# The last layer's output projection over pairs of token tiles: seven block products in place of eight

## The chip, the cores and the metric

The kernel runs on one core of one Trainium2 chip. The metric is the device time of one execution in microseconds (us), as the median of several executions. The core has five engines that run their own instruction streams and meet only at semaphores: TensorE (PE; PEld is its weight load), VectorE (DVE), ScalarE (ACT), GpSimd (POOL) and SyncE (SP), which here issues every DMA. Each engine works through its instructions in program order.

## The reference

Two layers of a streaming encoder over 2048 tokens of width 1024, and a final normalisation:

```python
for layer in range(2):
    hn = rms_norm(x, norm_gain[layer])
    aq, ak, av, ag, rq, rk, rv, rg = split(hn @ w_in[layer])      # eight parts of 512
    ya = chunked_rel_attention(aq, ak, av, rel_bias[layer])       # 8 heads x 64, band of 9 chunks of 64
    yr = chunkwise_retention(rq, rk, rv, cos, sin)                # 4 heads x 128, a running state
    y = concat([ya * silu(ag), yr * silu(rg)])
    x = x + y @ w_out[layer]                                      # the output projection: 2048x1024 by 1024x1024
return rms_norm(x, final_gain)
```

The change concerns `x + y @ w_out[layer]` of the second layer, and the final `rms_norm` that follows it.

## The kernel before

**Numbers in two halves.** Every matmul operand is split into two float16 halves, an upper one and the rest. A product takes three matmuls: upper by upper, upper by rest, rest by upper. ACT writes the upper half (a copy with a scale), DVE the rest (value times scale minus upper half).

**Stages.** For each layer and each of four head groups `s`, and each of four blocks `n` of 512 tokens, `dense_T` (L654) and `dense_V` (L785) project the input; the attention and retention of a block run beside the dense work of the next block. The generator `attention` (L823) has 24 steps; `run` (L1219) takes one of them for each step of the dense work, and spreads background work (`push`, `bg`) over the same steps: loading and splitting the next weights, for instance. The results of attention and retention go to `y_d` in device memory by tiles of 128 tokens. All four computing engines have their order written out by hand (`manual_schedule`); the SP queue's order is made by the framework, apart from DMAs marked `in_turn`.

**The output projection, `wout` (L1117).** It runs after the last dense block. The work goes over 16 token tiles of 128 rows, each in two halves of 512 output columns; one half is 8 blocks of 128 inner rows by three terms, 24 matmuls into one PSUM bank of the pool `psD` (two banks):

```python
for m in range(8 * (i % 3), 8 * (i % 3) + 8):
    kt, w = divmod(m, 3)
    h_, w_ = ((u.h, gc[c].vh), (u.h, gc[c].vl), (u.lo, gc[c].vh))[w]
    pe.matmul(ps, h_[:, kt, :], w_[:, kt, :], start=(m == 0), stop=(m == 23))
```

Six steps make a tile. After each half DVE adds PSUM times a scale to the residual tile (L1175). Ahead of that, a tile's `y` is loaded (`y_load` L967, SP), squared on ACT for its scale (`y_squares` L990), scaled by five small DVE operations (`y_scale` L999, `norm_scale`), split by `rows_hi` (ACT, L234) and `rows_lo` (DVE, L240), and transposed by two DMAs, one for each half (`y_turn` L1005, `transpose_rows` L243 and L244). POOL takes no part in this. `final` (L1013) does the last normalisation of a tile: squares on ACT (L212), a power on POOL (L219), a multiply on DVE (L1018) and the store (L1019). The last half of the last tile is cut into two quarters of 256 columns (L1159), finished by `final_half` (L1073). While the first tiles are projected, the last block's attention still runs, one of its 24 steps for each step of `wout`. The weights are split by `prep_O` (L551), once for each half of the columns, and the first tile's `y` is prepared by `wout_first` (L1096), all as background work of the last dense blocks.

Of the kernel before, what the change touches and what calls it, by code (L numbers as in the profile page):

```python
# [18 lines left out]
P = 128  # L19
# [8 lines left out]
def hybrid_trunk(ctx: ExitStack, tc: tile.TileContext, x, pos, gain, gcol, w_in, w_out, rel, fgain,  # L28
# [1161 lines left out]


    bg = []
    tab_done = set()

    def push(gen, steps):
        bg.append([gen, steps])
# [21 lines left out]

    def run(gen, att, thirds):  # L1219
        left = thirds  # L1220
        for _ in gen:
# [216 lines left out]
    for l in range(DEPTH):  # L1438
        gO = [Grp(), Grp()]
        go = Grp()  # L1440
        for s in range(NSW):
            g = grp(l, s)
            for n in range(NS):
# [25 lines left out]
                if n == (NS - 1 if (l, s) == (0, 0) else 1):  # L1469
                    if s + 1 < NSW:  # L1470
                        push(prep_T(l, s + 1, grp(l, s + 1)), 25 if (l, s) != (0, 0) else 19)
                    else:
# [6 lines left out]
                if last:  # L1479
                    us = []  # L1480
                    push(wout_first(l, go, us), 9)
                if not first:
                    run(dT, att, 12 if last else 10 if n == 0 else 18 if (l, s, n) == (0, 0, NS - 1) else 22 if (l, s) == (0, 0) else 24)
                if n == NS - 1:
                    if s + 1 < NSW:
                        push(prep_V(l, s + 1, grp(l, s + 1)), 23)
                    else:
                        push(with_turn(prep_O(l, 1, gO[1], go), us), 12)
# [8 lines left out]
        if l + 1 == DEPTH:  # L1497
            ring["fg"] = b3.tile([P, D], F32, tag="wh", name="fg")
            sp.dma_start(ring["fg"], fgain.to_broadcast([P, D]))
        wT = Sections(l + 1, 0, grp(l + 1, 0), True) if l + 1 < DEPTH else None  # L1500
        wo = wout(l, go, gO, us, wT)
# [78 lines left out]
```

## Time and profile before

| what | value |
|---|---|
| median of 3 runs | 2060.24 us (2058.01 to 2061.81) |
| span of the profiled execution | 2060.7 us |
| PE busy | 1999.4 us, 97% |
| DVE busy | 1228.1 us, 60% |
| ACT busy | 1134.8 us, 55% |
| POOL busy | 688.1 us, 33% |
| DMA, share of 16 engines, main queue | 65.6% |

The profiled execution's own time and its span are taken as one: 2060.7 us, which is 0.5 us (0.02%) above the median of the runs and inside their range.

How to read the rows: a group of instructions is given as line, engine, operation, output<-inputs, shape, count, then busy time in us and the mean ns of one, then the idle time of the engine in front of them. A row of the stretches of time gives for each engine its busy us and, in brackets, its instructions; then the granted TensorE clock, the DMA share and GB/s. A row of the timeline or of the chain starts with the time in us from the start of the span, then the duration. PE durations overlap: matmuls are pipelined, so that the distance of two starts is what one costs in a row of many.

### The profile page before, as it was taken

Reading aid. Unit: us, or ns where it says so; the run is one execution under the profiler, and the core shown is the slowest. Engines: PE = TensorE matmul, PEld = TensorE weight load, DVE = VectorE, ACT = ScalarE, POOL = GpSimd, SP = SyncE. Lnnn points to the kernel's source line nnn. Section 1 sums busy time; section 2 is a strip of 40 time slices with the busy share of each in tenths; the row PEclk is TensorE's granted clock in tenths of the full one; section 3 lists DMA queues with packets and bytes.
Section 4 is the critical chain, followed back from the end, with each engine's and each line's share of the span. In section 5 each row is a group of like instructions: output and inputs, shape, how many; then the busy total and the mean of one; then the engine's idle time right before and its main releaser. Section 6 shows DMA issues by size and latency. Waiting matters only on the chain. (4 is left out here: it accounts for less than half of the span.)

```text
span 2060.7 us, 39339 instructions
## 1 busy us (share of the span) xinstructions
PE 1999.4 (97%) x14038; PEld 1052.9 (51%) x14038; DVE 1228.1 (60%) x3804; ACT 1134.8 (55%) x2526; POOL 688.1 (33%) x701
## 2 busy tenths in 40 slices
PE   6988999999999999999999999999999999999998
PEld 4444555555555555554444555555555555555544
DVE  6776666565556555666553556555655566557643
ACT  6556665556565645555444546655656565455432
POOL 0344343434334434430003443444333334333100
PEclk9999999999999999999999999999999999999999
DMA  8778664547584754899774546554746775658864
GB/s 227 169 161 178 155 148 109 112 114 164 117 185 113 165 128 101 174 209 263 219 185 113 124 104 156 116 126 103 158 117 150 148 155 124 129 115 187 224 203 139
DMA packets 645701, 313.64 MB, mean 152 GB/s; under 512 B 459232, under 2 KB 602080, under 8 KB 645504
## 3 DMA queue, kind: packets, MB, share of 16 engines
q1 hardware_dynamic: 645504, 311.12, 65.6%
q8 instruction: 110, 1.80, 0.4%
q14 instruction: 87, 0.71, 0.1%
HBM read 123.26 MB, written 41.98 MB: 80 GB/s over the span
## 5 line engine op out<-in xcount | busy, mean ns | idle before, releaser
L855 POOL TENSOR_TENSOR pq<-sc,pq 128x640 f16<-128x640 f32 (+4 forms) x256 | 319.4, 1248 | 860.5 <-ACT pq L854 443.8
L852 ACT ACTIVATE sc<-sc,mq,cT 128x640 f32<-128x640 f32 (+4 forms) x256 | 218.4, 853 | 615.6 <-DVE rl L871 309.7
L797 PE MATMUL dV<-whV,hTh 128*128 128x512 f16 x1024 | 353.9, 381 | 7.3 <-DVE gt L815 6.1
L797 PE MATMUL dV<-whV,hTl 128*128 128x512 f16 x1024 | 353.8, 381 | 0.0
L797 PE MATMUL dV<-wlV,hTh 128*128 128x512 f16 x1024 | 353.8, 381 | 0.0
L778 PE MATMUL dT<-hTh,whT 128*128 128x512 f16 x1008 | 346.6, 379 | 2.7 <-DVE kk L697 1.3
L778 PE MATMUL dT<-hTl,whT 128*128 128x512 f16 x1008 | 346.6, 379 | 0.0
L778 PE MATMUL dT<-hTh,wlT 128*128 128x512 f16 x1008 | 346.6, 379 | 0.0
L797 PEld LDWEIGHTS <-hTh 128*128 128x128 f16 x2048 | 197.0, 98 | 224.7 <-DVE gt L815 10.0
L778 PEld LDWEIGHTS <-whT 128*128 128x128 f16 x2016 | 192.1, 98 | 207.7 <-issue 1.6
L849 DVE CUSTOM_DVE_ANT_0 sc<-S,bias 128x640 f32<-128x640 f32 (+4 forms) x256 | 188.3, 735 | 88.8 <-PE S L846 87.4
L1172 PE MATMUL dO<-whO,yly 128*128 128x512 f16 x504 | 191.0, 379 | 1.7 <-DMA yly<-hTl 1.1
L1172 PE MATMUL dO<-whO,yhy 128*128 128x512 f16 x504 | 191.0, 379 | 1.0 <-DMA yhy<-hTh 1.0
L1172 PE MATMUL dO<-wlO,yhy 128*128 128x512 f16 x504 | 191.0, 379 | 0.0
L854 ACT ACTIVATE pq<-sc 128x640 f16<-128x640 f32 (+4 forms) x256 | 171.5, 670 | 8.1
L797 PEld LDWEIGHTS <-hTl 128*128 128x128 f16 x1024 | 99.4, 98 | 112.4 <-issue 3.9
L1172 PEld LDWEIGHTS <-yhy 128*128 128x128 f16 x1008 | 98.1, 98 | 113.7 <-DMA yhy<-hTh 1.5
L778 PEld LDWEIGHTS <-wlT 128*128 128x128 f16 x1008 | 97.2, 98 | 113.7 <-issue 6.0
L845 PE MATMUL S<-k,q 128*128 128x128 f16 (+3 forms) x592 | 142.4, 267 | 0.0
L865 PE MATMUL o<-v,pT 128*128 128x65 f16 x1120 | 129.8, 193 | 6.4 <-DMA pT<-pq 5.5
L866 PE MATMUL o<-v,pT 128*128 128x64 f16 x1120 | 130.1, 195 | 0.0
L846 PE MATMUL S<-k,q 128*128 128x128 f16 (+3 forms) x592 | 129.7, 267 | 0.0
(359 smaller groups left out, 3476.5 us busy)
## 6 DMA issues: line engine op xcount, KB each, us to landing
q<-qq SPq DMA_DIRECT2D x128, 128.0 KB, 2.4
yyy<-y_d SPq DMA_DIRECT2D x32, 512.0 KB, 4.5
stT<-in_w_in_dram SPq DMA_DIRECT2D x27, 512.0 KB, 4.8
stV<-in_w_in_dram SPq DMA_DIRECT2D x26, 512.0 KB, 4.6
k<-kk SPq DMA_DIRECT2D x128, 64.0 KB, 2.0
swp<-rot SPq DMA_DIRECT2D x64, 128.0 KB, 3.1
tabc<-tab SPq DMA_DIRECT2D x32, 256.0 KB, 3.0
tabs<-tab SPq DMA_DIRECT2D x32, 256.0 KB, 3.1
```

The lines of the kernel that those rows point to most:

```text
L778: pe.matmul(ps, w_[:, j, kt, :], h_[:, kt, :], start=(m == 0), stop=(m == 23))
L797: pe.matmul(ps, h_[:, kt, a * P:(a + 1) * P], w_[:, kt, :], start=(m == 0), stop=(m == 23))
L845: pe.matmul(o, st.q[:, hx, 0, cs], k_, start=True, stop=False)
L846: pe.matmul(o, st.q[:, hx, 1, cs], k_, start=False, stop=True)
L849: dve.tensor_tensor_reduce(out=v, in0=S[:, 0:w], in1=g.bias[hx][:, 640 - w:640], scale=1.0, scalar=-3.0e38, op0=ALU.add, op1=ALU.max, accu ...
L852: act.activation(v, v, AF.Exp, bias=m[:, 0:1], scale=g.c[:, 0:1])
L854: act.activation(pq[:, 0:w], v, AF.Copy)
L855: pool.tensor_tensor(pq[:, w:2 * w], v, pq[:, 0:w], op=ALU.subtract)
L865: pe.matmul(o[:, 0:65], u.p[:, b, :], v_[:, 0:65], start=(b == 0), stop=False)
L866: pe.matmul(o[:, 0:64], u.p[:, b, :], v_[:, 65:129], start=False, stop=False)
L1172: pe.matmul(ps, h_[:, kt, :], w_[:, kt, :], start=(m == 0), stop=(m == 23))
```

## The change

The last layer no longer uses `wout`. Two token tiles make a pair: 256 rows, cut into two by two blocks A11, A12, A21, A22 (128 tokens by 512 inner columns). `w_out` is cut into two by two blocks of 512 by 512. Seven products of sums of such blocks replace the eight block products; each is 4 inner blocks by 3 terms, 12 matmuls of 128x512, so a pair takes 84 in place of 96. The sums of blocks are made in float32 before they are split into halves.

- `fast_weights` and a part of `pair_first` make seven weight blocks in place of four: sums and differences on POOL, then the split on ACT and DVE. The weights are loaded 12 times 512 KB in place of 8 times.
- `pair_first` prepares the first pair as background work of the last dense block, in 24 steps.
- `fast_out` runs 8 pairs, each in 12 rounds of 7 matmuls. In the same rounds it prepares the next pair by the list `plan`: squares, scales, multiplication in place (ACT, float32), five sums of blocks (POOL), and for each of seven blocks the upper half (`pair_rows`, ACT), the rest (`pair_lower`, DVE, one of them on POOL) and one DMA transpose of both halves (`pair_turn`). The row buffers are three tags used in turn.
- Each product goes into one or two of the four output blocks: `add_to` is the DVE operation as before; `by_copy` is a scaled copy on ACT and an addition on POOL.
- The attention that runs beside it takes one step for every second round (`run(..., 96, 2)`).

```diff
+    PRODS = (("A22", "D21"), ("A11", "D12"), ("S2", "B11"), ("S5", "B22"), ("S1", "T1"), ("S7", "T7"), ("S6", "T6"))
+    def fast_weights(l, fw, go):
...
+        for j in range(4):
...
+                st += load_sec(w_out[l, :, c * 512 + j * P:c * 512 + (j + 1) * P], f"F{l}_{j}{c}")
...
+                pool.tensor_tensor(tm[:, k * h:(k + 1) * h], st[0][:, k * h:(k + 1) * h], st[1][:, h:KT], op=ALU.add)
...
+            pool.tensor_tensor(st[0][:, h:KT], st[0][:, h:KT], st[0][:, 0:h], op=ALU.subtract)
+            pool.tensor_tensor(st[1][:, 0:h], st[1][:, 0:h], st[0][:, 0:h], op=ALU.add)
...
+    def pair_sq(u, k, junk):
...
+        act.activation(junk, u.y[k], AF.Square, accum_out=m)
...
+    def pair_mul(u, k):
+        act.activation(u.y[k], u.y[k], AF.Copy, scale=u.s[k][:, 0:1])
...
+    SUMS = {"S1": ("A11", "A22", ALU.add), "S2": ("A21", "A22", ALU.add), "S6": ("A21", "A11", ALU.subtract),
+            "S7": ("A12", "A22", ALU.subtract), "S5": ("A11", "A12", ALU.add)}
...
+        pool.tensor_tensor(part_of(u, nm), part_of(u, a), part_of(u, b), op=op)
+    def pair_rows(u, nm, space=None):
+        if space is None:
+            tag = ("tabc", "tabs", "swp")[rowring[0] % 3]
...
+        act.activation(space[:, 0:512], part_of(u, nm), AF.Copy)
+    def pair_lower(u, nm):
+        eng = pool if nm == "S1" and u.p else dve
+        eng.tensor_tensor(u.r[nm][:, 512:1024], part_of(u, nm), u.r[nm][:, 0:512], op=ALU.subtract)
+    def pair_turn(u, nm):
+        sp.dma_start_transpose(out=u.T[nm], in_=u.r[nm])
...
+    def fast_out(l, fw, go, u, areas):
...
+        mm = [(i, kt, w) for i in range(7) for kt in range(KT // 2) for w in range(3)]
+        plan = {0: (("sq", 0),), 1: (("sq", 1), ("scale", 0)), 2: (("scale", 1), ("mul", 0)), 3: (("mul", 1), ("rows", "A11")),
+                4: (("lower", "A11"), ("rows", "A22"), ("sum", "S2")),
+                5: (("turn", "A11"), ("lower", "A22"), ("rows", "S2"), ("sum", "S1"), ("sum", "S6")),
+                6: (("turn", "A22"), ("lower", "S2"), ("sum", "S7"), ("sum", "S5")),
+                7: (("turn", "S2"), ("rows", "S5")), 8: (("lower", "S5"), ("rows", "S1"), ("x", 0)),
+                9: (("turn", "S5"), ("lower", "S1"), ("rows", "S7"), ("y", 0)),
+                10: (("turn", "S1"), ("lower", "S7"), ("rows", "S6"), ("y", 1)),
+                11: (("turn", "S7"), ("lower", "S6"), ("turn", "S6"))}
...
+            def add_to(x_, c, ps, s_):
+                dve.scalar_tensor_tensor(out=half(x_, c), in0=ps, scalar=s_[:, 0:1], in1=half(x_, c), op0=ALU.mult,
+                                         op1=ALU.add)
+            def by_copy(x_, c, ps, s_, op):
...
+                act.activation(v, ps, AF.Copy, scale=s_[:, 0:1])
+                pool.tensor_tensor(half(x_, c), half(x_, c), v, op=op)
...
+                    pe.matmul(ps, u.T[an][:, kt + (4 if w == 2 else 0), :], fw.w[bn][1 if w == 1 else 0][:, kt, :],
+                              start=(m % 12 == 0), stop=(m % 12 == 11))
...
+                    if i == 0:
+                        add_to(x2, 0, ps, s2)
+                        by_copy(x1, 0, ps, s1, ALU.add)
+                    elif i == 1:
+                        add_to(x1, 1, ps, s1)
+                        by_copy(x2, 1, ps, s2, ALU.add)
+                    elif i == 2:
+                        add_to(x2, 0, ps, s2)
...
+                        by_copy(x2, 1, ps, s2, ALU.subtract)
+                    elif i == 3:
+                        add_to(x1, 1, ps, s1)
+                        by_copy(x1, 0, ps, s1, ALU.subtract)
+                    elif i == 4:
+                        add_to(x1, 0, ps, s1)
+                        add_to(x2, 1, ps, s2)
+                    elif i == 5:
+                        add_to(x1, 0, ps, s1)
+                        final(u.t, x1, at)
+                    else:
+                        add_to(x2, 1, ps, s2)
+                        final(u.t + 1, x2, at)
...
-    def run(gen, att, thirds):
+    def run(gen, att, thirds, slow=1):
...
-            if att[0] is not None and next(att[0], att) is att:
+            if att[0] is not None and i % slow == 0 and next(att[0], att) is att:
...
+                if (l + 1, s, n) == (DEPTH, NSW - 1, 2):
+                    push(fast_weights(l, fw, go), 24)
...
+                        push(pair_first(l, u0, fw, go, areas), 24)
...
+            run(fast_out(l, fw, go, u0, areas), att, 96, 2)
+            continue
```

The last product of the last pair is cut into two quarters of 256 columns with `final_half`, as the last half was before. `final` puts its three operations into later rounds (2, 3 and 5 rounds after the last addition); those that fall behind the last round are issued after everything else.

More of the change, by code (lines that the diff above doesn't have):

```diff
@@ L1497, in hybrid_trunk @@
         if l + 1 == DEPTH:
-            ring["fg"] = b3.tile([P, D], F32, tag="wh", name="fg")
+            ring["fg"] = cp.tile([P, D], F32, tag="gb", name="fg")
             sp.dma_start(ring["fg"], fgain.to_broadcast([P, D]))
+            run(fast_out(l, fw, go, u0, areas), att, 96, 2)
+            continue
         wT = Sections(l + 1, 0, grp(l + 1, 0), True) if l + 1 < DEPTH else None
```

225 lines of the change are left out of this document (220 added, 5 removed).

## Prediction

> **What bounds the kernel now.** I read the page's busy times first, then stretches of time, the chain of work that ended last, and the timelines of single engines around the projection. The chain's last long piece and the stretches carry the argument.
>
> ```profile
> 1820.00:1874.00 54.00, 54.00 (x414) 29.08 (x413) 33.54 (x96) 32.86 (x69) 23.68 (x19) 1.00 0.68 135
> 1876.20:1936.70 60.50, 60.18 (x468) 32.41 (x466) 43.02 (x127) 33.47 (x67) 17.40 (x18) 1.00 0.93 219
> 1936.80:2049.00 112.20, 112.20 (x522) 50.95 (x521) 48.69 (x106) 33.48 (x50) 6.02 (x11) 1.00 0.65 190
> ```
>
> ```profile
> 1936.74 112.25 PE dO L1172 x520
> ```
>
> ```profile
> 1873.60 0.38 PE L797 MATMUL dV<-wlV,hTh 128*128 128x512 f16 x1
> ...
> 1876.25 0.38 PE L1172 MATMUL dO<-whO,yhy 128*128 128x512 f16 x1
> ```
>
> The stretches are, in order, the last dense block, the projection with attention beside it, and the projection alone. PE (first column after the length) is full in all three, DVE, ACT and POOL (third to fifth) are not, and the clock is 1.00. So PE is the bound of the projection, and what one matmul costs is 112.25 us / 520 = 0.216 us. It runs from 1876.25 to 2054.2 us, where the tail (quoted below) begins: 178 us. Of this 744 x 0.216 + 48 quarter matmuls x 0.11 (half of 0.216) = 166 us are its own, so 12 us are attention's. Two tiles cost 96 x 0.216 = 20.7 us.
>
> **What the change removes.** 12 of 96 matmuls in each of 8 pairs: 96 x 0.216 = 20.7 us of PE. A pair becomes 84 x 0.216 = 18.1 us. That is the whole possible gain, if PE stays the bound.
>
> **What it adds to the other engines.** Prices, ACT first (timeline; then one line's instructions with minimum, median and maximum in ns):
>
> ```profile
> 1958.24 1.15 ACT L234 ACTIVATE hTh<-yyy,sy 128x1024 f16<-128x1024 f32 x1 [4.68 <-DVE iy L153]
> 1961.78 1.03 ACT L212 ACTIVATE fj<-hTl 128x1024 f32<-128x1024 f32 x1 [2.39 <-DVE hTl L1175]
> ...
> 1962.84 1.04 ACT L997 ACTIVATE hTh<-yyy 128x1024 f16<-128x1024 f32 x1
> ```
>
> ```profile
> L711 ACT ACTIVATE raw<-dT x32: 571/597/597, 54.2 to 1847.9; 128x512 f32<-128x512 f32 x32
> ```
>
> ```profile
> L724 ACT ACTIVATE rot<-raw x32: 612/613/631, 81.7 to 1870.5; 128x512 f16<-128x512 f32 x32
> ```
>
> In a row of ACT instructions a 1024-wide square costs 1.06 us from start to start, so about 0.1 us of each overlaps the next; a scaled 1024-wide copy 1.05, a 512-wide copy out of PSUM 0.6, a 512-wide float16 row 0.52 (0.61 alone).
>
> POOL and DVE:
>
> ```profile
> 1851.21 1.27 POOL L719 TENSOR_TENSOR rot<-rot,tabc 128x512 f32<-128x512 f32 x1 [1.88 <-PE S L846]
> 1852.44 1.28 POOL L720 TENSOR_TENSOR swp<-swp,tabs 128x512 f32<-128x512 f32 x1
> 1853.79 1.27 POOL L721 TENSOR_TENSOR rot<-rot,swp 128x512 f32<-128x512 f32 x1
> ...
> 1864.74 2.26 POOL L719 TENSOR_TENSOR raw<-raw,tabc 128x512 f32<-128x512 f32 x1
> ```
>
> ```profile
> L727 DVE TENSOR_TENSOR rot<-raw,rot x32: 678/1423/1477, 82.4 to 1871.1; 128x512 f16<-128x512 f32 x32
> ```
>
> ```profile
> L1018 DVE SCALAR_TENSOR_TENSOR hTl<-hTl,rsf,fg x7: 1274/1277/2318, 1926.2 to 2050.8; 128x1024 f32<-128x1024 f32 x7
> ```
>
> ```profile
> L1175 DVE SCALAR_TENSOR_TENSOR hTh<-dO,oscy,hTh 128x512 f32<-128x512 f32 x16 | 12.0, 750 | 32.0 <-PE dO L1172 32.0
> ```
>
> ```profile
> L219 POOL TENSOR_TENSOR rsf<-ssf,mhalf 128x1 f32<-128x1 f32 x15 | 8.2, 547 | 107.5 <-DVE ssf L217 107.5
> ```
>
> A 512-wide float32 addition on POOL takes 1.27 us, three of them one behind the other 3.8. `pair_lower` has the form of L727: 0.68 us undisturbed, but mostly 1.4; L719 and L1018 also have a long form, 1.0 us longer. These are the times when DVE and POOL both work on SBUF and one waits for the other. `add_to` is L1175, 0.75.
>
> The DMAs (issue to landing in us, first beside attention, then alone):
>
> ```profile
> yyy<-y_d SPq DMA_DIRECT2D x6, 512.0 KB, 3.9
> ...
> yhy<-hTl SPq DMA_TRANSPOSE x2, 3.7
> ```
>
> ```profile
> yyy<-y_d SPq DMA_DIRECT2D x8, 512.0 KB, 4.4
> ...
> yhy<-hTl SPq DMA_TRANSPOSE x5, 3.1
> ```
>
> ```profile
> 1960.76 1.23 SPq L243 DMA_TRANSPOSE yhy<-hTh  x1
> ```
>
> SP is held for 1.23 us by each transpose.
>
> Sums of busy time for a pair of `fast_out`: POOL 10 additions x 1.27 + 2 powers x 0.55 = 13.8 us. ACT 4 squares, 2 multiplications, 7 rows, 4 copies = 4.2 + 2.1 + 3.6 + 2.4 = 12.3. DVE 8 x 0.75 + 6 x 0.68 + 2 x 1.28 + twelve small ones at 0.15 = 14.4. No engine's sum passes 18.1. What decides is their order, because each engine takes them in turn and they hand the same blocks back and forth.
>
> **The loop.** The program order gives for ACT in one pair: four squares (two of the finished pair, two of the next y), copy 1, two multiplications, rows A11, copy 2, rows A22, rows S2, copies 3 and 4, rows S5, S1, S7, S6, then the next pair's squares. For POOL: addition 1, addition 2, sums S2, S1, S6, addition 3, sums S7, S5, addition 4. Count from the first square, T = 0. ACT: squares to 4.2, copy 1 to 4.8, multiplications to 6.9, rows A11 to 7.4, copy 2 to 8.0. POOL cannot do addition 2 before, and S5 is the seventh operation from there: 8.0 + 7 x 1.27 = 16.9. Rows S5 on ACT to 17.5; the rest of S5 on DVE to 18.2 undisturbed, to 18.9 if POOL's addition 4 is in the way; its transpose lands 3.1 to 3.4 later, 21.3 to 22.3. Rows S6 use the row buffer that this transpose empties (three buffers in turn, S6 is third after S5): 21.9 to 22.9. Only then ACT starts the next squares. PE is not in this loop, it waits at its edge. A second way to the same point agrees: after the rest of S5, DVE does two additions of product 5, the rest of S7 and the addition of product 6 (0.75 x 3 + 0.68) and the square of that tile can start at 21.2 to 21.9.
>
> A third: on SP the load of the second y tile stands behind the transposes of S5 and S1, whose rest POOL finishes at 19.4; issued at about 21.3 it lands at 25.2 to 25.7, when its square is due at 22.4 + 3.2 = 25.6. It is just hidden.
>
> So a round trip is 22.4 us where nothing collides, against 18.1 for PE and 20.7 for two tiles before. In the stretch from copy 2 to S5, DVE has one 1.28 us multiplication and three rests to do, all beside POOL at work: 0 if they fall into gaps, 1.0 + 3 x 0.68 = 3.0 if each holds POOL up. I take 1.6, the middle, since L727 is long in more than half its cases: 24.0 us. With attention (four pairs, since it takes a step in every second round) ACT has more to do ahead of copy 2:
>
> ```profile
> 1881.86 0.92 ACT L852 ACTIVATE sc<-sc,mq,cT 128x640 f32<-128x640 f32 x1 [1.85 <-DVE rl L871]
> ...
> 1883.93 0.25 ACT L903 ACTIVATE dT<-r 128x128 f16<-128x128 f32 x1
> ```
>
> That is one unit of attention and one of retention, 2.3 us, and 0.2 for a state: 26.5 us; 1 us more if its POOL work is in the way too. The first pair lacks two squares: 24.4.
>
> A rule of the Trainium skill bears on the collisions (SBUF — State Buffer, Who interferes with whom): a VectorE instruction with two SBUF inputs and a GpSimd instruction that reads SBUF exclude each other for the whole instruction. The trace agrees: L727 at 0.68 or up to 1.48. By that rule alone, with POOL's 13.8 and DVE's 6 x 0.68 + 2 x 1.28 = 6.6 laid end to end, a pair could not go under 20.4 us, and six trips of 3.6 us less would make 2054.
>
> **The sum**, against the span of 2060.7 (0.5 above the median, so the same). Start of the loop: ACT must have emptied the last dense product. It does so late, behind an exponential that waited for DVE:
>
> ```profile
> 1879.69 0.31 ACT L808 ACTIVATE rv<-rv 128x128 f16<-128x128 f16 x1
> ```
>
> so 1879.9 (1875.3 if this lag goes). Six round trips, 24.4 + 3 x 26.5 + 2 x 24.0 = 151.9, then S5 of the last pair lands at 23.4: 2055.2. PE then has four products: 36 x 0.216 + 24 x 0.11 = 10.4, so 2065.6. The tail:
>
> ```profile
> 2054.28 0.46 DVE hTl L1162
> ...
> 2054.85 0.52 ACT fj L1079 x2
> 2055.39 0.17 DVE ssf L1085
> 2055.67 0.58 POOLq L1576
> 2056.27 0.75 DVE hTl L1091
> ```
>
> From 2054.2 to 2060.7 it is 6.5 us. The change adds to it: the last pair's first tile is normalised wholly behind the last rounds, so ACT's square (1.12), a small DVE operation, a power (0.55) and a multiplication (1.28) stand behind the last scaled copy in place of L1091's 0.75: 3.1 us more. Together 2075.2.
>
> The weights and the first pair are prepared in the last two dense blocks: POOL 16 + 4 + 5 operations x 1.27 = 32 us, ACT and DVE some 15 us and 11 us more than before, 4 loads more. The first stretch above shows the cover (DVE 62%, ACT 61%, POOL 44%), so I take 1 us, between 0 and 6, the lag of ACT quoted above (1879.7 less 1873.6) if it came once more. The forecast is 2076 us.
>
> **The rivals.** PE stays the bound: the handovers overlap better than my order says. For it: sums under 18.1 on every engine and PE full today. Against: the loop above needs no engine to be full. Start as before at 1876.25, 660 x 0.216 + 2.6 + 12 = 157.2, tail 9.6: 2043, faster. It decides where a round trip without attention comes under 18.1; any gain needs it under about 20.7.
>
> The loop at its lower ends: no collision, landing 3.1, no lag: 22.0 + 3 x 24.1 + 2 x 21.9 + 21.3 = 159.4 from 1875.3, plus 20.0: 2054.7; with the lag 2059. No measurable change, or little gain.
>
> DMA comes late: a transpose of 256 KB and the 512 KB moves filled 0.65 x 10.36 = 6.7 us per tile; by the first transpose of a tile,
>
> ```profile
> 1961.40:1963.60 2.20, 2.20 (x12) 1.02 (x11) 1.65 (x3) 1.82 (x3) 0.34 (x1) 1.00 0.64 119
> ```
>
> 1.4 us each, a move 1.3. A pair of the change has 7 and 6: 17.7 us, 98% of PE's 18.1. Beside attention a share of 0.93 did no harm above, and the loop gives 24. If landings still grew by 1.8 us in six trips: 2087.
>
> **How the numbers follow.** Loop with collisions 0.62 (2065 to 2096: upper end from 22.9 + 3.0 a trip and 1 us more beside attention, most of it together), lower ends 0.15, PE bound 0.13, late DMA 0.10. A measurement tells about 0.2%, 4 us, from no change: the lower ends split into 0.12 same and 0.03 faster. Faster 0.16, same 0.12, slower 0.72. The range 2054 to 2096 leaves out PE bound and a little above.
>
> **What would show it.** After: PE with gaps in `fast_out`, ended by transposes of row blocks; POOL in runs of seven operations; rows S5 on ACT waiting for POOL; starts of the first square 22 to 25 us apart after attention; `pair_lower` near 1.4 us. Wrong if PE is full there, or if the trips are near 18.

## The result

| | before | after |
|---|---|---|
| median of 4 runs each (lowest to highest) | 2060.48 us (2058.01 to 2061.81) | 2152.01 us (2151.64 to 2157.42) |
| span of the profiled execution | 2060.7 us | 2150.3 us |
| last dense product ends | 1874.0 us | 1897.5 us |
| projection, first to last product | 178.0 us | 236.0 us |
| from there to the end | 6.5 us | 13.3 us |

The changed kernel takes 1.0451 times as long (95% interval 1.0436 to 1.0467), 4.5% more. The forecast was 2076 us with a range up to 2096: the sign was right, the size far too small. The 89.6 us between the spans are 23.5 in front of the projection, 1.2 until its first product, 58.0 in it and 6.8 behind it.

Three views of the changed kernel answer those of the prediction. First its stretches: the last three dense blocks (two of values, one of the transposed projections), a round trip beside attention, one without, and the whole projection. Columns as before: length, then busy us and instructions of PE, PEld, DVE, ACT and POOL, granted clock, DMA share, GB/s.

```profile
1794.90:1897.50 102.60, 83.48 (x602) 42.80 (x599) 63.13 (x154) 56.14 (x113) 64.89 (x52) 0.97 0.62 144
1973.70:2009.60 35.90, 23.37 (x138) 11.67 (x138) 22.49 (x46) 16.91 (x31) 19.43 (x15) 0.79 0.64 161
2071.20:2097.60 26.40, 20.96 (x88) 8.88 (x87) 17.02 (x28) 13.12 (x23) 15.32 (x12) 0.87 0.77 190
1901.00:2137.00 236.00, 173.00 (x926) 81.56 (x923) 147.18 (x292) 114.67 (x200) 130.97 (x103) 0.88 0.67 168
```

Before, PE filled every such stretch. Now nothing does: in the trip beside attention PE has 23.4 us of 35.9, POOL 19.4, DVE 22.5. This is the sign of a loop of waits. It also stands in the dense blocks, where PE has only 83.5 of 102.6 us.

Second, ACT's timeline: the first square of each trip.

```profile
1907.03 1.04 ACT L1256 ACTIVATE yTh<-yyz 128x1024 f16<-128x1024 f32 x1
...
1937.87 1.01 ACT L212 ACTIVATE fj<-hTh 128x1024 f32<-128x1024 f32 x1
...
1973.65 1.01 ACT L212 ACTIVATE fj<-hTl 128x1024 f32<-128x1024 f32 x1
...
2009.63 1.01 ACT L212 ACTIVATE fj<-hTh 128x1024 f32<-128x1024 f32 x1
...
2044.96 1.01 ACT L212 ACTIVATE fj<-hTl 128x1024 f32<-128x1024 f32 x1
...
2071.25 1.01 ACT L212 ACTIVATE fj<-hTh 128x1024 f32<-128x1024 f32 x1
...
2097.58 1.01 ACT L212 ACTIVATE fj<-hTl 128x1024 f32<-128x1024 f32 x1
```

The differences are the six round trips: 30.8, then 35.8, 36.0 and 35.3 with attention, then 26.3 and 26.3.

Third, one trip of each kind. Without attention (from 2071.25), ACT:

```profile
2073.54 1.06 ACT L1256 ACTIVATE yTh<-hTh 128x1024 f16<-128x1024 f32 x1 [1.16 <-DMA hTh<-y_d]
...
2081.01 0.69 ACT L1438 ACTIVATE cpz<-zz,oscz 128x512 f32<-128x512 f32 x1 [0.67 <-DVE hTl L1431]
...
2092.12 0.63 ACT L1296 ACTIVATE rwz_6S<-hTh 128x512 f16<-128x512 f32 x1 [3.56 <-POOL hTh L1286]
...
2097.05 0.63 ACT L1296 ACTIVATE rwz_6S<-hTl 128x512 f16<-128x512 f32 x1 [3.26 <-DMA yTh<-rwz_6S]
```

This is the loop of the prediction, link by link: copy 2 (2081.01), rows S5 waiting for POOL, rows S6 waiting for the transpose that empties its row buffer, and then the next squares at 2097.58. Beside attention (from 1973.65), ACT's copy 2 and rows S6, DVE's rest of S5, and SP:

```profile
1985.86 0.69 ACT L1438 ACTIVATE cpz<-zz,oscz 128x512 f32<-128x512 f32 x1 [1.37 <-DVE hTh L1431]
...
2009.09 0.63 ACT L1296 ACTIVATE rwz_3S<-yyz 128x512 f16<-128x512 f32 x1 [10.23 <-DMA yTh<-rwz_3S]
```

```profile
1997.86 1.09 DVE L1300 TENSOR_TENSOR rwz_3S<-yyz,rwz_3S 128x512 f16<-128x512 f32 x1 [2.93 <-ACT rwz_3S L1296]
```

```profile
2000.23 1.33 SPq L857 DMA_TRANSPOSE pT<-pq  x1
2001.65 1.02 SPq L1310 DMA_DIRECT2D hTl<-x_d  x2
2002.76 0.38 SPq L880 DMA_DIRECT2D y_d<-ya  x1
2003.20 1.32 SPq L1303 DMA_TRANSPOSE yTh<-rwz_3S  x1
```

The rest of S5 is ready at 1998.95, but SP issues its transpose only at 2003.20. In front of it stand attention's transpose (whose rest of probabilities POOL makes behind the four additions and five sums, up to 2000.2), two loads of the next residual and a store. And it lands 5.9 us after its issue instead of 3.1, with 1 MB of loads in front of it. ACT waits 10.23 us.

In the dense blocks, the waits of the last three of them, and one place in ACT's and PE's order:

```profile
ACT hTh L1220 <- POOL stF L1215: 10.1, 3, 4.1
...
ACT hTh L1329 <- POOL stG L1326: 6.1, 3, 4.4
DVE rwz_0S L1300 <- ACT rwz_0S L1296: 5.2, 1, 5.2
```

```profile
1801.28 1.15 ACT L1220 ACTIVATE hTh<-stF,o_s 128x1024 f16<-128x1024 f32 x1 [4.10 <-POOL stF L1215]
...
1804.20 0.38 PE L797 MATMUL dV<-whV,hTh 128*128 128x512 f16 x1 [2.17 <-ACT raw L711]
```

ACT waits for POOL's sums of weights (L1215) and differences (L1326). Behind ACT's waiting split stand the eviction of the dense product (L711) and attention's exponentials, and PE waits for these: in the two rows, ACT waits 4.10 us for POOL, and behind this and two splits PE waits 2.17 us for the eviction.

### The profile page after: what moved, and what is told of

It reads as the page before. It is cut to its first block, busy times and chain, and to the rows that moved or that the text cites. A ratio compares the mean times of both kernels' runs of the same rounds, so it can differ in the third digit from the quotient of the medians.

```text
span 2150.3 us, 39602 instructions
## 1 busy us (share of the span) xinstructions
PE 1998.6 (93%) x13930; PEld 1046.4 (49%) x13930; DVE 1297.6 (60%) x3877; ACT 1192.0 (55%) x2622; POOL 827.3 (38%) x800
## 5 line engine op out<-in xcount | busy, mean ns | idle before, releaser
L797 PE MATMUL dV<-whV,hTh 128*128 128x512 f16 x1024 | 353.3, 381 | 12.1 <-DVE gt L815 9.4
L865 PE MATMUL o<-v,pT 128*128 128x65 f16 x1120 | 130.5, 194 | 18.0 <-DVE ssf L217 9.9
L865 PEld LDWEIGHTS <-pT 128*128 128x128 f16 x1120 | 106.0, 97 | 55.8 <-DMA pT<-pq 12.9
L952 POOL TENSOR_TENSOR rss<-rss,mhalf 128x1 f32<-128x1 f32 x128 | 74.8, 585 | 147.1 <-DVE rss L951 139.0
L867 PE MATMUL o<-v,pT 128*128 128x65 f16 x1120 | 129.9, 193 | 0.0
L811 DVE SCALAR_TENSOR_TENSOR v<-dV,v 128x128 f16<-128x128 f32 x128 | 36.5, 285 | 140.6 <-ACT rv L807 129.8
```

Source lines behind the costliest of these rows:

```text
L797: pe.matmul(ps, h_[:, kt, a * P:(a + 1) * P], w_[:, kt, :], start=(m == 0), stop=(m == 23))
L865: pe.matmul(o[:, 0:65], u.p[:, b, :], v_[:, 0:65], start=(b == 0), stop=False)
L867: pe.matmul(o[:, 0:65], u.p[:, u.nb + b, :], v_[:, 0:65], start=False, stop=(b == u.nb - 1))
L952: pool.tensor_tensor(ss, ss, mhalf, op=ALU.pow)
```

## The experiments

Trips are read between the first squares of two finished pairs, as above. "With" and "without" are trips with attention beside them and the first two after it (in e6 five). Where no interval is given, a time is that of one run. The runs come from four chips (e1 to e4, e5 to e8, e9 to e12, e13 to e15), on which the kernel before took 2064.2, 2060.3, 2060.6 (median of seven, 2060.0 to 2064.1) and 2059.0 us. So differences of about 5 us between the times of single runs are not told from noise; trips, which are read inside one trace, are the firmer measure.

| run | with | without | time |
|---|---|---|---|
| changed kernel | 35.8, 36.0, 35.3 | 26.3, 26.3 | 2152.0 |
| e1_own_junk | 35.0, 35.3, 34.3 | 26.5, 26.7 | 2150.7 |
| e2_four_rows | 35.1, 34.8, 34.5 | 32.1, 26.6 | 2145.9 |
| e3_dve_adds | 32.6, 32.6, 32.6 | 24.6, 24.3 | 2131.1 |
| e5_x_late | 36.7, 36.0, 35.8 | 32.1, 31.3 | 2177.3 |
| e6_attention_first | | 26.6, 26.2, 26.6, 26.1, 26.7 | 2160.8 |
| e9_loads_early | 29.3, 29.5, 29.5 | 24.9, 25.8 | 2120.5 |
| e10_best | 28.9, 25.6, 25.6 | 23.2, 23.4 | 2094.3 |
| e13_best_no_x | 28.9, 25.6, 25.6 | 21.1, 19.5 | 2087.8 |
| e14_best_no_x_y | 28.9, 25.6, 25.6 | 21.1, 19.5 | 2086.6 |
| e15_no_x | 31.8, 32.3, 32.3 | 27.1, 26.6 | 2141.6 |

### Four single causes

e1: the final squares write their unused output into own memory, not into the PSUM tile that attention's scores share.

```diff
-            return squares(xt, f"f{t}", psS.tile([P, D], F32, tag="S", name=f"fj{t}"))
+            return squares(xt, f"f{t}", psS.tile([P, D], F32, tag="S", name=f"fj{t}") if junk is None else junk)
...
-                        final(u.t, x1, at)
+                        final(u.t, x1, at, u.T["S2"].rearrange("p k c -> p (k c)"))
```

> In the changed kernel the trips of ACT (first square to first square) take 35.8, 35.9 and 35.4 us while attention runs beside them and 26.2 and 25.9 us after it, and PE stands idle 13 us in each of three trips ahead of a score matmul that waits for ACT's square of the finished tile. Both use the one PSUM tile S. Here the final squares write into SBUF space of the finished pair in place of that tile; nothing else changes. Theory A (the shared tile puts PE and attention into ACT's loop): the three trips fall to 27 to 30 us, the 13 us gaps go, the total falls by 18 to 26 us to 2125 to 2134. Rival B (attention's own work in the queues of ACT, DVE and POOL makes the trips long): the gap moves to another wait, the trips stay at 34 or more, and the total falls by less than 5 us.

Measured: 2150.7 us, trips shorter by 1 us at most. In the changed kernel PE waits 4.9, 13.0 and 12.6 us for that square in the three trips (not 13 in each, as I had written); here the wait stands at another place:

```profile
PE zz L1469 <- DVE ya L877: 10.0, 1, 10.0
ACT rwz_3S L1296 <- DMA yTh<-rwz_3S: 9.8, 1, 9.8
```

PE waits at the edge of the loop for whatever comes next; ACT's wait for the transpose stayed. So the shared tile was not the cause.

e2: a fourth row buffer, so that rows S6 do not need the one that the transpose of S5 empties.

```diff
-            tag = ("tabc", "tabs", "swp")[rowring[0] % 3]
+            tag = ("tabc", "tabs", "swp", "qq")[rowring[0] % 4]
```

> The row buffers go round over four tags in place of three, so that rows S6 wait for the transpose of S2 and not of S5. Theory A (the loop is closed by several ways that end close together): a trip without attention falls by 0.5 to 1.5 us, since the square then waits for DVE's addition of product 6 or for the y load; total 4 to 12 us lower, 2140 to 2147. Rival C (the wait for a row buffer alone closes the loop): a trip falls by the 3.3 us that ACT waits there, the total by 20 us or more.

Measured: 2145.9 us, 6 us less, inside theory A's range but little above the noise. ACT's wait for that transpose is gone, and rival C's 20 us did not come. The expected gain without attention did not come either: those trips take 26.6 us, as before. (The 32.1 in the table is a shift: the first square of a trip now runs up to 12.5 us ahead of the second finished tile's square, 5.3 in the changed kernel. Between the squares of the second tile the five trips are 34.8, 34.5, 32.1, 26.6 and 26.3, and in the changed kernel 35.8, 36.0, 32.6, 27.0 and 25.4.) Behind the link the same order of work holds the next squares up (waits for loads of y of 1.92 and 0.87 us, and 2.17 us for DVE's addition). Taken alone it closes no gap.

e3: all additions on DVE straight from PSUM, so that the copies on ACT and the four additions on POOL go; `ns` are the negated scales, one small DVE operation a tile.

```diff
-                act.activation(v, ps, AF.Copy, scale=s_[:, 0:1])
-                pool.tensor_tensor(half(x_, c), half(x_, c), v, op=op)
+                add_to(x_, c, ps, s_ if op == ALU.add else ns[0] if s_ is s1 else ns[1])
```

> The four additions of a pair that went by an ACT copy and POOL are done by DVE straight from PSUM, as the other eight are; POOL keeps the sums of blocks. Theory A (the chain of seven POOL operations from the second copy to S5 sets the trip): POOL's chain starts after the second multiplication and has five operations, S5 comes 5 to 6 us earlier, a trip without attention takes 20 to 22 us in place of 26; total 25 to 45 us lower, 2107 to 2126. Rival D (DVE is the tighter engine: its 14.4 us get 3 us more): trips stay within 1.5 us of 26, total within 10 us of 2152.

Measured: 2131.1 us, 21 us less, the largest gain of a single edit, though short of the 25 to 45 expected. POOL's last sum S5 now starts at T + 13.9 us and ends at T + 15.5 (T = 2057.9) where it ended at T + 20.8:

```profile
2064.41 1.30 POOL L1289 TENSOR_TENSOR S2z<-hTl 128x512 f32<-128x512 f32 x1 [1.29 <-ACT hTl L1271]
...
2071.77 1.59 POOL L1289 TENSOR_TENSOR hTh<-hTh 128x512 f32<-128x512 f32 x1
```

But the trip fell by 2 us only and not by 5: the transpose of S5 is now issued at 2074.97, right behind the two loads of the residual, and ACT waits 5.3 us for it. So the end of POOL's queue was one link of the bound, and the landing of the transposes is the next.

e4: the 16 sums of weights on POOL left out.

```diff
-            tm = w4.tile([P, KT, P], F32, tag="w4", name=f"tmF{l}_{j}")
-            for k in range(2):
-                pool.tensor_tensor(tm[:, k * h:(k + 1) * h], st[0][:, k * h:(k + 1) * h], st[1][:, h:KT], op=ALU.add)
             yield
-            pool.tensor_tensor(st[0][:, h:KT], st[0][:, h:KT], st[0][:, 0:h], op=ALU.subtract)
-            pool.tensor_tensor(st[1][:, 0:h], st[1][:, 0:h], st[0][:, 0:h], op=ALU.add)
-            srcs = (st[0], st[1], tm)
+            srcs = (st[0], st[1], st[0])
```

> Leaves out the sixteen sums of weight blocks on POOL in the preparation of the last two dense blocks (three of the seven weight blocks then hold plain blocks of w_out and the output is not the reference's); the splits on ACT and DVE, the loads and all of the rest stay. The second last dense block's second half takes 35.6 us in the changed kernel and 25.8 in the one before, the last block 65.4 against 51.8. Theory E (ACT and DVE stand in their queues behind POOL's sums, and with them the softmax and the emptying of PSUM): the first goes back to 26 to 28 us, the last block, whose own POOL work stays, gains little; total 7 to 12 us lower. Rival F (the splits themselves overload DVE and ACT): less than 3 us.

Measured: 2138.6 us, 13.4 us less. The last dense product ends at 1882.1 instead of 1897.5. The last three dense blocks take 90.5 us, in the changed kernel 102.6 and in the kernel before 78.0, so 12.1 of the 24.6 us lost in them go; the projection is as long as in the changed kernel (236.4 us). POOL's sums held the dense blocks, by making ACT wait. They did not do it where theory E had them: the block of values, which was to go back to 26 to 28 us, still takes 32.4 (35.6 in the changed kernel), and the last block, which was to gain little, takes 57.7 us instead of 65.3.

### Order on SP, and attention

e5: the loads of the residual moved behind the transposes.

```diff
-                7: (("turn", "S2"), ("rows", "S5")), 8: (("lower", "S5"), ("rows", "S1"), ("x", 0)),
+                7: (("turn", "S2"), ("rows", "S5")), 8: (("lower", "S5"), ("rows", "S1")),
...
-                11: (("turn", "S7"), ("lower", "S6"), ("turn", "S6"))}
+                11: (("turn", "S7"), ("lower", "S6"), ("turn", "S6"), ("x", 0))}
```

> Only the place of the two loads of the next pair's residual tiles changes: from in front of the transpose of S5 on SP to behind the last transpose of the pair. Theory (order on SP): in the changed kernel the transpose of S5 was ready at 1998.05 us, issued at 2002.28 behind attention's transpose and the two loads, and landed at 2007.8. Without the loads ahead of it a round trip beside attention falls from 35.8 us by 2 to 4 us, one without attention from 26 by 0 to 1, and the time by 6 to 14 us. Rival (the loads stand there for nothing, SP only waits for attention's own transpose): trips within 1 us of before, time within 3 us. If the residual now comes late for the first addition of a pair, the trips get longer, and POOL's first addition is seen waiting for these loads.

Measured: 2177.3 us, 25 us slower. The case that the expectation named last came, with DVE and not POOL as the first to wait:

```profile
ACT cpz L1438 <- DVE hTl L1431: 6.3, 3, 4.7
...
DVE hTl L1431 <- DMA hTl<-x_d: 6.2, 1, 6.2
```

DVE's first addition waits 6.2 us for the residual, ACT's copy stands behind it, and the whole loop starts later. The loads can't go back; they can only go forward.

e6: attention to its end before the projection.

```diff
+            def only_attention():
+                while att[0] is not None:
+                    yield
+            run(only_attention(), att, 24)
             run(fast_out(l, fw, go, u0, areas), att, 96, 2)
```

> The last block's attention runs to its end before the projection starts; nothing else is changed. Theory (attention's own work stands in the queues of ACT, DVE, POOL and SP between the links of the loop): trips 1 to 3 fall from 35.8 us to the 26 us of trips 4 and 5, trip 0 from 27.3 to 23 to 25, so the projection from its first to its last product takes 236 - 32 = about 204 us. Rival (the first trips are long for another reason, the clock or the row buffers): trips 1 to 3 stay over 31 us. The whole time says little, since the attention now stands by itself: 24 steps alone of perhaps 2 to 4 us each, less the 32 us.

Measured: all trips 26.1 to 26.7 us, trip 0 24.6, the projection 205.6 us against 236.0. The theory holds: attention beside the loop cost 30 us. By itself it cost more: from the last dense product to the first of the projection it is now 46.4 us instead of 3.5, which is why the time rose to 2160.8.

e7: the diffs of e1, e2, e3 and the late loads of e5 together.

> Four edits together: all additions on DVE straight from PSUM (no copies on ACT, no additions on POOL), a fourth row buffer, the final squares into own memory in place of the shared PSUM tile, and the loads of the residual behind the transposes. Theory (loop through the queues): with DVE's additions S5 was summed at T + 15.4, and its transpose then lost 3 us behind two loads; without these it lands about 19 to 20 after T, and with the fourth row buffer the next squares need not wait for it: trips without attention 20 to 23 us (24.5 with DVE's additions alone), with attention 27 to 31 (32.6), time 2095 to 2118 us. Rival (the DMAs set the trip by their sum, 17.7 us of them in a pair beside attention's): trips without attention stay at 24 or more, time over 2120 us.

Measured: 2153.7 us. Since the late loads alone cost 25 us, it tells nothing of the others; its trips, 34.1 to 35.9 us with attention, 30.6 and 28.6 without, are those of late loads on a shorter loop. Neither its theory (2095 to 2118 us) nor its rival, the sum of the DMAs, is settled by it.

e8: as e4, and the rests of six weight blocks left out too.

```diff
+        for _, lo in big:
+            dve.memset(lo, 0.0)
+            yield
...
-                if i > 0:
-                    dve.scalar_tensor_tensor(out=big[i - 1][1][:, :, js], in0=srcs[i - 1], scalar=go.os[:, 0:1],
-                                             in1=big[i - 1][0][:, :, js], op0=ALU.mult, op1=ALU.subtract)
```

> The 16 sums of the weights on POOL and the lower halves of six of the seven weight blocks (12 operations on DVE) are left out, three fills on DVE in their place; the output is not the reference's. Theory (the dense blocks lose their 25 us because each instruction of the preparation stands in the queue between links of the dense work): without the sums alone 12 us were won; without the lower halves as well 16 to 22 us, the last two value blocks at 27 to 30 us each. Rival (the rest of the loss is the loading and the first pair's preparation): no more than 14 us, the value blocks stay at 31 to 32 us.

Measured: 2138.7 us, no better than e4, where 4 to 10 us more were expected. The block of values before the last fell from 32.4 to 27.9 us, but the next two took it back (27.3 and 33.9 against 25.7 and 31.6), and the block ahead of them took 26.6 instead of 25.6, with the three fills in it. The rests on DVE are not the rest of the loss. What the last block still shows are the first pair's differences and sums on POOL, for which ACT waits:

```profile
DVE hTl L1328 <- ACT hTh L1324: 6.1, 1, 6.1
ACT hTh L1324 <- POOL stG L1321: 5.7, 2, 4.4
...
ACT rwz_0S L1291 <- POOL hTh L1281: 3.6, 1, 3.6
```

### The best order

e9: e3, and the loads forward.

```diff
+        plan = {0: (("sq", 0),), 1: (("sq", 1), ("scale", 0), ("y", 0)), 2: (("scale", 1), ("mul", 0), ("y", 1)), 3: (("mul", 1), ("rows", "A11")),
...
+                6: (("turn", "A22"), ("x", 0), ("lower", "S2"), ("sum", "S7"), ("sum", "S5")),
```

> The kernel with all additions on DVE, and the loads moved forward: the two residual tiles from in front of the transpose of S5 to behind that of A22, the two y tiles of the pair after next from the end of the round trip to its start (the previous run showed that moved back they cost 5 us a trip, 6.2 us of it in DVE's wait for a residual tile). Theory (the transpose of S5 took 6.7 us because 1 MB of loads lay in front of it in the DMA queues): it lands 3 to 4 us after its issue, trips without attention fall from 24.5 to 21.5 to 23 us, with attention from 32.6 to 29.5 to 32, the time from 2131 to 2110 to 2124 us. Rival (the DMAs are the bound by their sum, wherever they stand): trips stay at 24 us or more, time over 2126 us.

Measured: 2120.5 us, inside the theory's range, but for half of its reason. Trips with attention fell by 3 us, those without did not (24.9, 25.8). There ACT waits 6.8 us at rows S7, whose row buffer the transpose of S2 empties: now the transposes of S2 and S5 stand together behind the 1 MB and need 7.8 us. The DMA share of that trip is 0.85.

e10: e9, the fourth row buffer of e2, own memory for the squares as in e1, and all sums for the weights and for the first pair on DVE as in e11.

> As the run before it, and a fourth row buffer, own memory for the final squares, and the sums for the weights and for the first pair on DVE in place of POOL. Theory: the dense blocks win 10 to 18 us (POOL's sums no longer hold ACT's splits), a trip 0 to 1.5 us, time 2090 to 2112 us: still slower than the 2060 of the kernel before, since attention's trips stay near 30 us and the tail near 9.5. Rival (DVE takes POOL's place as the bound of the dense blocks): not more than 4 us better than the run before it.

Measured: 2094.3 us (2091.1 to 2098.4), 1.0158 times the kernel before (interval 1.0138 to 1.0178). 58 of the 92 us lost are won back, and the kernel before is still 1.6% faster. The last dense product ends at 1889.2. As e2 and e1 are in it together, what each of the two gives here is not shown.

e11: only the sums of weights and of the first pair on DVE.

```diff
-            pool.tensor_tensor(st[0][:, h:KT], st[0][:, h:KT], st[0][:, 0:h], op=ALU.subtract)
+            dve.tensor_tensor(st[0][:, h:KT], st[0][:, h:KT], st[0][:, 0:h], op=ALU.subtract)
```

> One edit to the changed kernel: the 16 sums of weights, the 4 differences and the first pair's 5 sums are DVE's in place of POOL's, nothing is left out. Theory (the 25 us of the dense blocks are ACT's and DVE's waits for POOL, whose sums stand behind each other and behind the rotary operations, 12.9 and 6 us of waits of ACT in the profile): the last dense product ends at 1880 to 1887 instead of 1897.5, the time falls by 10 to 18 us. Rival (it is the amount of work beside the dense blocks, whoever does it): the blocks stay at 33 us or more and the time falls by less than 5 us, or rises.

Measured: 2142.8 us, 9.2 less; the last dense product ends at 1887.7. Both lie just outside the theory's ranges (10 to 18 us, 1880 to 1887). Both sides are partly right: ACT's waits for POOL's sums are gone from the view, but its exponentials wait more for DVE:

```profile
ACT sc L852 <- DVE mq L851: 38.2, 11, 8.4
```

(26.2 us in the changed kernel). The work moved from one queue in which it stood in the way to another.

e12: e10 with attention taking a step in every round.

```diff
-            run(fast_out(l, fw, go, u0, areas), att, 96, 2)
+            run(fast_out(l, fw, go, u0, areas), att, 96, 1)
```

> The best combination with attention taking a step in every round instead of every second one, so that two trips carry it instead of four. Theory (each step of attention lengthens the loop that it stands in by its place in the queues, about 1.5 us a step): two trips of 36 to 42 us and four of 21 to 23, time within 6 us of the best combination. Rival (a trip with attention is long because of one wait in it, whatever the number of steps): two trips near 30 us, and the time 14 to 20 us less.

Measured: 2099.7 us, 5.5 more than the median of e10 and 1.4 above its slowest run. The six trips take 29.1, 33.5, 23.7, 21.7, 21.8 and 23.4 us, together 153.1 against 149.4. Attention costs about the same however it is spread, as the theory says, though its two trips are shorter than the 36 to 42 expected.

### Is it the DMAs?

e10 still has trips of 23.4 us, far over PE's 18.1. The last three runs leave loads out: e13 those of the residual from e10, e14 those of y as well (the same condition in `pair_y`, with the first odd pair's tiles used again), e15 those of the residual from the changed kernel.

```diff
-            in_turn(sp.dma_start(u.x[k], x_d[u.t + k]))
+            if u.p < 2:
+                in_turn(sp.dma_start(u.x[k], x_d[u.t + k]))
```

> The combination of the best order, with the two loads of the residual left out from the third pair on (the tiles of the pair before the last are added to again; the output is not the reference's). Theory (the DMA engines are the bound now): the share of the DMAs stays near 0.9 and a trip falls by about the time of two moves, 2.6 us: 21 us without attention (23.4), 23 with (25.6), time 2078 to 2084 us. Rival (the order on POOL, ACT and SP bounds it): the share falls to 0.8, trips within 0.8 us of before, time over 2088 us.

> As the run before it, and the two loads of y left out as well from the third pair on (the tiles of the pair before the last are scaled again). Theory (DMA the bound): with 4 of 13 moves gone, about 5.2 us, the DMAs need 15.4 us a trip and cease to be the bound; PE with 18.1 us, or the order, takes over: trips of 18.5 to 21 us, time 2063 to 2080 us. Rival (order): trips stay at 22 to 23.4, time over 2085 us.

> The changed kernel with the two loads of the residual left out from the third pair on. Theory (its own trips stand on the order of the queues, and on these loads only where they lie in front of the transpose of S5): trips with attention fall by 1 to 4 us from 35.8, those without by 0 to 2 from 26.3, the time by 6 to 16 us, far less than the best order wins. Rival (the DMAs bound the changed kernel too): trips without attention fall by 2.6 us or more, the share of the DMAs stays near 0.77.

Measured: 2087.8, 2086.6 and 2141.6 us. A trip without attention in e10, e13 and e14:

```profile
2024.50:2047.90 23.40, 20.59 (x96) 9.02 (x94) 17.87 (x34) 10.17 (x18) 9.94 (x8) 1.00 0.88 217
```

```profile
2021.80:2041.30 19.50, 19.50 (x92) 8.78 (x91) 17.84 (x36) 10.31 (x17) 9.93 (x8) 1.00 0.86 207
```

```profile
2020.40:2039.90 19.50, 19.50 (x92) 8.80 (x90) 17.84 (x35) 10.35 (x18) 9.94 (x8) 1.00 0.70 153
```

Without the residual's loads the two trips fall by 2.1 and 3.9 us, where two moves are 2.6. So in the best order it is the DMAs that hold a trip without attention, through the 1 MB in the same few microseconds as the transposes (S2 and S5 land after 6.9 us in e10, after 3.5 in e13). Leaving out the y loads too frees the DMAs (0.86 to 0.70) and changes nothing. Neither answer as I had put it is whole: the theory expected a further gain from the y loads, and there is none.

What holds the trip of 19.5 us then is not PE. PE is full in the row of e13, but with 92 matmuls, 8 more than a pair has; in the trip after it, as long, it is busy for 18.4 of 19.5 us, and in neither does another engine wait for it. The square that starts the trip waits for DVE:

```profile
2041.32:2060.79 19.47, 18.42 (x86) 8.26 (x85) 17.80 (x35) 10.31 (x17) 9.93 (x8) 1.00 0.70 155
```

```profile
2038.01 0.69 DVE L1304 TENSOR_TENSOR rwz_6S<-hTh,rwz_6S 128x512 f16<-128x512 f32 x1 [0.50 <-ACT rwz_6S L1300]
2038.62 1.40 DVE L1437 SCALAR_TENSOR_TENSOR hTl<-zz,oscz,hTl 128x512 f32<-128x512 f32 x2
2039.94 0.68 DVE L1304 TENSOR_TENSOR rwz_6S<-hTl,rwz_6S 128x512 f16<-128x512 f32 x1
2040.54 0.74 DVE L1437 SCALAR_TENSOR_TENSOR hTl<-zz,oscz,hTl 128x512 f32<-128x512 f32 x1
```

```profile
2041.32 1.06 ACT L212 ACTIVATE yTh<-hTl 128x1024 f16<-128x1024 f32 x1 [1.15 <-DVE hTl L1437]
```

These are the rest of S5, two additions, the rest of S7 and the addition of product 6, one behind the other: the second way to the next squares that the prediction named. With the transposes out of the way, the order of ACT, POOL and DVE is still a loop of 19.5 us, longer than PE's 18.1. Trips with attention stayed at 25.6 in all three, at DMA shares of 0.93, 0.81 and 0.65: those are held by the order on ACT, DVE and POOL, not by the DMAs.

In the changed kernel itself (e15) the same loads cost 3 to 4 us in a trip with attention and nothing in one without: there the order of the queues was the bound, as the theory said.

The ordering within one queue that this rests on is stated by the Trainium skill (DMA: Bandwidth & Descriptors, Queues, rings and completion order): on each DMA engine the descriptors of a queue are taken in ring order. The trace agrees: transposes behind the loads land in 5.9 us (S5, changed kernel with attention) to 7.8 (S2 and S5, e9), and in 3.0 to 3.5 where the loads are done or left out (changed kernel without attention, e13).

## Why the prediction was wrong

The mechanism was the one seen: PE not the bound, a loop from the squares over POOL's chain to S5, its transpose and the row buffer, PE waiting at its edge. Of what was to be seen, PE's gaps, POOL's run of seven operations, rows S5 waiting for POOL and a rest of 1.1 to 1.75 us came; the trips of 22 to 25 us after attention did not. "PE stays the bound" and "the loop at its lower ends" did not happen. The sum was wrong by 74 us, in these terms (the forecast's direction came true, but by costs that it had put at almost nothing):

| step of the prediction | predicted | measured | off |
|---|---|---|---|
| start of the loop (1879.9 + 1) | 1880.9 | 1907.0 | +26.1 |
| trip 0 | 24.4 | 30.8 | +6.4 |
| three trips with attention | 79.5 | 107.1 | +27.6 |
| two trips without | 48.0 | 52.6 | +4.6 |
| S5 of the last pair and four products | 33.8 | 39.4 | +5.6 |
| tail | 9.6 | 13.3 | +3.7 |

**"So I take 1 us, between 0 and 6."** This step failed most plainly: it is 23.5 of the 26.1 us in the first row. I took engines at 44 to 62% as cover for 32 us of POOL's work. But a share says nothing of an order: each sum of POOL stands in front of a split on ACT, and ACT's split in front of the evictions and exponentials that PE waits for. The profile had the shape of this already (ACT's exponential waiting for DVE, POOL's rotary work in rows of three). e4 shows 12 us of it as the weights' sums; by the ends of the last dense product (1882.1 in e4, 1887.7 in e11, 1889.2 in e10, against 1874.0) 8 to 15 us remain when the sums are gone or moved. In every run the last block of values took 29.8 us or more (25.8 in the kernel before) with the first pair's preparation in it; no run took that preparation away, so this part is argued and not shown.

**"26.5 us; 1 us more if its POOL work is in the way too."** The prediction's own links, set against the trip from 1973.65: copy 2 was due at T + 10.5 and ended at T + 12.9 (+2.4: attention's exponential and split, and DVE's addition in front of it). POOL's chain took 10.5 us, as predicted with collisions. The rows and the rest of S5 took 1.8 where I had 1.3 (+0.5). Then SP: I had counted no wait there, and it was 4.25 us. And the landing took 5.9 us in place of 3.1 to 3.4 (+2.6). Together +9.75; the trip was 9.5 longer than forecast. I had counted what attention adds to ACT, and mentioned POOL, but not SP's queue, though SP takes its DMAs in turn as the engines take their instructions. e6 shows 30 us as the price of attention in the loop, where I had four times 2.5, and e15 3.0 to 4.0 us of each trip as the residual's loads. Trip 0 has the same wait: 9.88 us at its rows S6.

**"It is just hidden."** The y load was not: copy 2 in a trip without attention ended at T + 10.4 and not at 8.0, of which 1.46 us are waits for the two y tiles and 0.67 for DVE's addition. This is the whole miss of the trips without attention, 26.3 against 24.0. The collisions, for which I took 1.6 us, came to 1.4 (10.3 us for seven operations of 1.27). POOL's sums take 1.71 us beside DVE's rests of 1.74, and 1.26 when DVE waits:

```profile
2083.25 1.71 POOL L1286 TENSOR_TENSOR S2z<-hTl 128x512 f32<-128x512 f32 x1
2084.92 1.71 POOL L1286 TENSOR_TENSOR S1z<-hTh,hTl 128x512 f32<-128x512 f32 x1
...
2090.82 1.26 POOL L1286 TENSOR_TENSOR hTh<-hTh 128x512 f32<-128x512 f32 x1
```

```profile
2083.76 1.74 DVE L1300 TENSOR_TENSOR rwz_6A<-hTl,rwz_6A 128x512 f16<-128x512 f32 x1
```

The Trainium skill's rule on the port that VectorE and GpSimd share (SBUF — State Buffer, Who interferes with whom) points the same way. That the two wholly exclude each other the trace does not show: a sum and a rest together took 1.67 us from start to start, less than the 1.27 and 0.68 that they take alone.

**"DMA comes late"** (0.10, 2087 us) was the rival nearest to the truth in its mechanism, as a part of the loop and not in its place. Its price was low: I worked out 17.7 us of DMA work in a pair; the share says 0.77 x 26.4 = 20.3 us in the changed kernel and 20.6 in e10. That is as much as the 20.7 us of PE that two tiles took before. So with its moves as they are, even the best order would hardly have gained: the work taken off PE came back as transposes and loads. This last step is an inference from the shares, not a run. The nearest run is e13, where two of the moves are left out and a trip still takes 19.5 us.

**The last pair.** The product of its S5 started 28.3 us after the last first square where I had 23.4, and the four products took 11.1 us where I had 10.4.

**The tail.** Predicted 9.6, measured 13.3. The 3.1 us in my 9.6 are the four new operations in full; without the 0.75 us that they were to replace, as I wrote, it would have been 2.35. Most of the miss is a wait: DVE's addition waits 2.97 us for POOL's, which stands behind a multiplication that waits for ACT's square.

```profile
2137.68 2.07 DVE L1431 SCALAR_TENSOR_TENSOR hTl<-zz,oscz,hTl 128x512 f32<-128x512 f32 x3 [2.97 <-POOL hTl L1439]
```

In e3, e9 and e10, where DVE adds everything, the tail is 9.5 to 9.9 us, near what the prediction had for an undisturbed one, though by a sum that was 0.75 too high.

## What to carry to other kernels

A change that takes work off the full engine and gives it to idle ones has to be costed by the order in which the idle ones hand it on, the queue that issues the DMAs among them: here 20.7 us of PE work were saved, and by the links of ACT, DVE, POOL, SP and DMA the time still rose by 90. "It fits beside, the engine is at 60%" is no argument in a stage where each added instruction stands in front of one that the full engine waits for. And the DMA time of a stage is worth a sum of its own, with measured prices, before the queues are looked at: it can tell that a gain isn't there.

## What was unexpected of the hardware

**Transposes fill the DMA engines at half the bytes.** In e14 from 2036 to 2037 only transposes run, in e13 from 2033 to 2034 the end of two stores:

```profile
2036.00:2037.00 1.00, 1.00 (x6) 0.42 (x5) 0.49 (x2) 1.00 (x3) 0.00 (x0) 1.00 0.96 187
```

```profile
2033.00:2034.00 1.00, 1.00 (x6) 0.42 (x5) 1.00 (x2) 0.00 (x0) 0.08 (x1) 1.00 1.01 410
```

The engines are full in both, at 187 and 410 GB/s. A transpose of 256 KB costs them about as much as a move of 512 KB.

**The granted clock fell with PE's idle time.** It was 1.00 in the whole projection before, 0.79 in the trip with a PE wait of 13 us, 0.87 with one of 5.3, and 1.00 again in e10's trip without attention, whose longest was 1.7; with attention alone (e6) 0.58. The Trainium skill (TensorE: Matmul & The Clock Gate, Why this matters for your kernels) warns of gaps of over about 3 us between bursts of matmuls; the trace agrees. What it cost can't be told from these runs: PE was not the bound where its clock was low, and e10's trip without attention took 23.4 us at 1.00.
